# Modulation rows of a two-layer diffusion step: column chunks one by one, or four at a time

## The chip, the cores and the metric

The kernel runs on one core of one Trainium2 chip. The time is the device time of one execution in microseconds (us); the median of several executions counts, and lower is better.

## The reference

One denoising step runs two trunks (128 context tokens and 128 latent tokens of 1024 features) through two layers. Each layer scales and shifts its rows by modulation vectors that come from a conditioning row, mixes the tokens with two recurrences (HGRN2 and mLSTM), adds the result through a gate, normalises, and runs a feed-forward product: a dense SwiGLU in layer 0, a top-2-of-8 mixture of experts in layer 1. Everything is float32. What the change touches is the modulation:

```python
act = jax.nn.silu(cond)
for l in range(DEPTH):
    mod = jnp.einsum('bd,dn->bn', act, w_ada[l]) + b_ada[l]     # w_ada[l]: 1024 x 6144
    sh1, sc1, g1, sh2, sc2, g2 = jnp.split(mod[:, None, :], 6, axis=-1)
    y, states = mixer(x * (1 + sc1) + sh1, ...)
    x = layer_norm(ALPHA * x + g1 * y, ln1_g[l], ln1_b[l])
    hh = x * (1 + sc2) + sh2
    f = swiglu(hh, ...) if l % 2 == 0 else moe_swiglu(hh, ...)
    x = layer_norm(ALPHA * x + g2 * f, ln2_g[l], ln2_b[l])
```

There are two conditioning rows, one for each trunk, so `mod` is a product of 2 rows with a matrix of 24 MB per layer.

## The kernel before, in words

**The large products.** A weight matrix comes from HBM in pieces of 256 rows x 512 columns (tile `ws`, 512 KB, a ring of three buffers). ScalarE (ACT) copies a piece to a rounded part `wh`, VectorE (DVE) subtracts it to get the rest `wl`, and TensorE (PE) takes three products of the two parts with the two parts of the rows (`hTh`, `hTl`) into a bank of PSUM. `gemm_fm` makes 512 output features of both trunks that way with 96 matmuls, `gemm_tm` does it with tokens on the partitions. Every DMA is issued by one queue, SyncE's (SP), in one order: a DMA that waits for its buffer holds back all that stand behind it.

**The modulation rows.** The 6144 columns of `w_ada[l]` are cut into 12 chunks of 512 (`cc` 0 to 11). `ada(l, cc)` makes one chunk. It loads the 1024 rows in four DMAs of 256 rows x 512 columns (tile `wa`, 512 KB; two buffers in pool `wp`, and every third load goes to one more buffer in the pool of the moment, by the list `extra`), and does eight matmuls, one for each tile `kt` of 128 rows. The stationary operand is `actT[:, kt]`, the silu of the conditioning, 32 columns wide of which 2 are used; the moving operand is the 128 x 512 piece of weights. Row tile `kt` goes to column group `kt % 4` of the array, so that each of the four groups (32 columns each, and 32 partitions of the PSUM bank each) holds the sum of two row tiles. `ps` is copied to `part` in SBUF, and four small matmuls (`adT`) with the selector `selc` add the four groups up and turn the chunk to feature-major; VectorE adds the bias and writes `mod`. Of the chunks that are gates (4, 5, 10, 11) the rows stay as rows: one matmul (`adR`) with the selector `selg` adds the groups and the bias row, which a DMA puts into partition 2 of `part`, and two rows of 512 go to HBM.

**When.** The first four chunks of layer 0 are made at the start, from weights loaded whole (`front`). The other 20 stand in the list `todo`; `chunk_done`, called at the end of every `gemm_fm` and `gemm_tm`, takes one entry. In layer 0's mixer there are 17 entries for 24 products, in the dense feed-forward four (chunks 0 to 3 of layer 1), in layer 1's mixer 16. PSUM bank `ad` of pool `adp` is one buffer: `ad`, `adT`, `adR`, the vectors' transposes `rT` and the products `warm` share it in turn. The framework's scheduler then sets the order of the instructions on every engine.

Names in the views: `ad` are the eight matmuls of a chunk, `mm` and `fp` the large products, `pl`, `po` those of the HGRN2 recurrence, `pn`, `pS`, `pqk`, `pC` those of the mLSTM. A float32 matmul stands in the trace as two records.

Of the kernel before, what the change touches and what calls it, by code (L numbers as in the profile page):

```python
# [17 lines left out]
T = 128  # L18
# [23 lines left out]
def backbone(ctx, tc, x_prompt, x_sample, c, state_hgrn, state_mlstm_C, state_mlstm_n, state_mlstm_m,  # L42
# [34 lines left out]
    tt(selg, selc[:, 0:2], ident[:, 2:3].to_broadcast([128, 2]), ALU.add)  # L77

# [66 lines left out]
    # conditioning: silu of both rows, as the stationary operand of the modulation product  # L145
# [7 lines left out]
    # lower bounds of the second layer's forget gates  # L153
# [34 lines left out]
    def sub(out, a, b):  # L188
        """a - b; GpSimd takes the first few after a norm, where the vector engine is what is waited for"""
        if aside[0]:  # L190
            aside[0] -= 1
            G.tensor_tensor(out, a, b, op=ALU.subtract)
        else:
            tt(out, a, b, ALU.subtract)
# [54 lines left out]
    def keep_warm(n, after=None):  # L249
        """Products that nothing reads, so that the array's clock stays up while a norm is waited for"""  # L250
        if not n:
            return
        with tc.issue_after(after or last_mm[0]):
            ps = adp.tile([128, 128], F32, tag="ad", name="warm")
            for _ in range(n):
                mm(ps, ident, ident)
# [3 lines left out]
    def chunk_done():  # L260
        """After a chunk of a product, a chunk of the modulation rows that are due later."""
        if todo:
            nxt = todo.pop(0)
            if callable(nxt):
                nxt()
            elif nxt:
                ada(*nxt)

# [5 lines left out]
    extra = []  # a pool with room for one more chunk  # L274
    chunks = [0]

    def ada_load(l, cc, k, pool=None, bufs=2):
        if extra and not pool:
            chunks[0] += 1
            if chunks[0] % 3 == 0:  # L280
                pool, bufs = extra[0], 1
        st = (pool or wp).tile([128, 2, 512], F32, tag="wa", name="wa", bufs=bufs)
        nc.sync.dma_start(out=st, in_=w_ada[l][k * 128:k * 128 + 256, cc * 512:cc * 512 + 512]
                          .rearrange("(k p) n -> p k n", p=128))
        return st

    def ada(l, cc, whole=None):
        """One chunk of 512 modulation values; the rows' tiles go to the four column groups in turn."""
        ps = whole[1].tile([128, 512], F32, tag="ad", name="ad") if whole else adp.tile([128, 512], F32, tag="ad", name="ad")
        for kt in range(KT):  # L290
            if kt % 2 == 0:
                st = whole[0][kt // 2] if whole else ada_load(l, cc, kt)
            g = kt % 4
            mm(ps[32 * g:32 * g + 32], actT[:, kt, :], st[:, kt % 2], kt < 4, kt >= 4, (0, 32 * g))
        part = wp.tile([128, 512], F32, tag="part", name="part", bufs=1)
        S.copy(part, ps)
        if cc in (4, 5, 10, 11):
            nc.sync.dma_start(out=part[2:3], in_=b_ada[l:l + 1, cc * 512:cc * 512 + 512])
            pf = adp.tile([2, 512], F32, tag="ad", name="adR")
            mm(pf, selg, part)  # L300
            S.copy(part[0:2], pf)
            nc.sync.dma_start(out=gates_d[l][cc // 6][:, (cc % 2) * 512:(cc % 2) * 512 + 512], in_=part[0:2])
            return
        end = None
        pf = (whole[1] if whole else adp).tile([128, 4, 2], F32, tag="xc" if whole else "ad", name="adT")
        for j in range(4):
            end = mm(pf[:, j], part[:, j * 128:j * 128 + 128], selc[:, 0:2])
        if whole and cc == 0:
            vectors(0, v1_first)
        tt(mod[l][:, 4 * cc:4 * cc + 4], pf,  # L310
           v1[l][:, 80 + 4 * cc:84 + 4 * cc, None].to_broadcast([128, 4, 2]), ALU.add)
        return end

    def mod_gb(l, which, g, b, ks=slice(0, 8)):
        """Scale and shift that take the normalised rows to the modulated ones."""
        n = ks.stop - ks.start
        sh = mod[l][:, 24 * which + ks.start:24 * which + ks.stop]
        sc = mod[l][:, 24 * which + 8 + ks.start:24 * which + 8 + ks.stop]
        gs = const.tile([128, n, 2], F32, name=f"gs{l}{which}{ks.start}")
        bs = const.tile([128, n, 2], F32, name=f"bs{l}{which}{ks.start}")  # L320
        V.tensor_scalar(gs, sc, 1.0, None, op0=ALU.add)
        if g is None:
            V.tensor_copy(bs, sh)
        else:
            tt(bs, gs, b[:, :, None].to_broadcast([128, 8, 2]), ALU.mult)
            tt(bs, bs, sh, ALU.add)
            tt(gs, gs, g[:, :, None].to_broadcast([128, 8, 2]), ALU.mult)
        return gs, bs
# [19 lines left out]
    def modulate(src, gs, bs, hm):  # L348
        """hm[feature, tile, trunk, token] = src^T * gs + bs"""
# [35 lines left out]
    def gate_rows(pool, tag, l, which, bufs=1):  # L385
        """A gate of each trunk over all partitions: [token, trunk, feature]"""
        gb = pool.tile([128, 2, D], F32, tag=tag, name="gb", bufs=bufs)
        for tr in range(2):
            nc.sync.dma_start(out=gb[:, tr], in_=bcast_row(gates_d[l][which][tr], D))
        return gb  # L390

    def norm_stats(small, row):
        """Mean and inverse deviation of a row [token, feature]"""
# [7 lines left out]
    def layer_norm(small, pre, trs=(0, 1)):  # L401
        """pre [token, trunk, feature] -> normalised, in place"""
# [6 lines left out]
    def norm_row(pool, tag, ap, bufs=1):  # L409
        """A norm's gain or bias over all partitions"""  # L410
# [15 lines left out]
    # ------------------------------------------------------------------ mixer  # L426
    def mixer(l, rhs, mx, sm, hp, mp, quads):
# [10 lines left out]
        # gates of the memory, rows [head, ...]  # L438
# [94 lines left out]
        def hgrn(g):  # L533
# [44 lines left out]
            def update(l2, ca=0, ck=0, step=1):  # L578
                """Blocks of 2**l2 become blocks of twice the size; of every step-th sequence, from ca and ck."""
# [38 lines left out]
            # outputs, normalised over each head  # L618
# [20 lines left out]
            def states():  # L639
                """Final states of the first trunk"""  # L640
# [25 lines left out]
        def gate_out(pp, y, norm, gate):  # L666
            """y [token, c, v] -> (y^T * norm gain * gate), feature-major, in gate's place"""
# [44 lines left out]
        def mlstm(g, raw, V1):  # L712
# [9 lines left out]
            for j in range(4):  # L722
# [35 lines left out]
                # sums of the gates over all partitions  # L758
# [35 lines left out]
                # final states of the first trunk  # L794
# [12 lines left out]
            # normalise over each head  # L807
# [58 lines left out]
    def residual(z, gb, q4, tr, ps):  # L866
        """z <- ALPHA * x + gate * ps for one half row of a trunk"""
# [4 lines left out]
    def quad(pool):  # L872
        """Two tensors of eight tiles"""
        t_ = pool.tile([128, 2, HC, T], F32, tag="mws", name="quad", bufs=4)
        return t_[:, 0], t_[:, 1]
# [35 lines left out]
    # ------------------------------------------------------------------ layer 0  # L911
    with tc.tile_pool(name="first", bufs=1) as first, tc.tile_pool(name="firstp", bufs=2, space=PSUM) as firstp:
        w_first = {}

        def front(cc):
            w_first[cc] = [ada_load(0, cc, k, first, 16) for k in range(0, KT, 2)]
# [36 lines left out]
        for q4 in range(2):  # L953
            ada(0, q4, (w_first[q4], firstp))
            x_cols(q4)
            end = ada(0, 2 + q4, (w_first[2 + q4], firstp))
# [14 lines left out]
    todo += [lambda: vectors2(0), (0, 4), lower]  # L971
    for cc in range(5, 12):
        todo += [(0, cc), vectors_rest if cc == 5 else None]
    mrhs = mixer_half(0, rhs0)
    assert not todo
    with ExitStack() as es:
# [9 lines left out]
        todo += [(1, cc) for cc in range(4)]  # L986
# [36 lines left out]
    # ------------------------------------------------------------------ layer 1  # L1023
    for cc in range(4, 12):
        todo += [None, (1, cc)]
# [24 lines left out]
    # router  # L1050
# [25 lines left out]
    with tc.high_priority():  # L1076
# [30 lines left out]
        # each token's place in its experts' lists  # L1107
# [5 lines left out]
    # modulated rows, token-major, in two parts  # L1113
# [27 lines left out]
    def park(src, kts, c0, tags=("gh", "gl"), bufs=6):  # L1141
        """Loads into the places of the gated rows that come after them"""
# [11 lines left out]
    def blocks(srcs, nk, c0, n, kinds=()):  # L1154
        """128 rows of n columns of every source at a time, side by side, in two parts"""
# [52 lines left out]
    def before_norm(tr, gate, out, q4):  # L1208
        """ALPHA * x + gate * the experts' sum, for half of a trunk's rows"""
# [5 lines left out]
    def finish(tr, mv, rstd, ng, out):  # L1215
        """The last norm of a trunk's rows"""
# [8 lines left out]
    def expert_weights():  # L1225
        """The chosen experts' weights"""
# [11 lines left out]
    def experts(first_slot):  # L1238
        """The tokens in slots first_slot..first_slot+127 of every expert's list."""
# [4 lines left out]
        def gather(p2):  # L1244
            """The rows of two experts' tokens, feature-major, and the places to put theirs back"""
# [149 lines left out]
```

## Time and profile before

| | |
|---|---|
| times of three executions | 1945.79, 1949.02, 1949.86 us; median 1949.02 |
| span of the profiled execution | 1946.4 us (of its time, the views give the span alone) |
| PE busy | 1882.5 us, 97% of the span |
| DVE busy, ACT busy | 1485.5 us (76%), 1186.7 us (61%) |
| chain that ended last, by engine | PE 91%, DVE 4%, DMA 3%, ACT 1%, issue 1% |
| mean DMA rate | 257 GB/s |

A matmul's end in the trace is modelled, and matmuls overlap; so what a matmul costs is read here from the start of one to the start of the next. A row of the timeline merges equal instructions that follow each other, gives the first one's start, and the time to the last one's end.

In time, the span falls into the start (0 to about 40 us), layer 0's mixer (to about 437), its output product and norm, the dense feed-forward (475 to 615 at its densest, to 693 with the norm), layer 1's mixer (to about 1090), router, and the experts (to the end).

### The profile page before, as it was taken

What the parts mean: (1) busy time and instruction counts of PE and PEld (TensorE: products, weight loads), DVE (VectorE), ACT (ScalarE), POOL (GpSimd) and SP (SyncE); (2) the same over time, 40 slices, a digit from 0 to 9 for tenths busy, and PEclk for the clock granted to TensorE, in tenths of its full rate; (3) what the DMA queues carried; (4) which work ended last, traced back from release to release, by engine and by line L of the source; (5) the groups of instructions that cost most, each with busy time, mean ns of one, the idle gap of its engine ahead of it and who ended that gap; (6) DMA issues with size and microseconds to landing.
All of it is one profiled execution on the core that took longest, in us unless ns stands there. A gap on an engine that the chain in (4) does not pass through costs nothing.

```text
span 1946.4 us, 31146 instructions
## 1 busy us (share of the span) xinstructions
PE 1882.5 (97%) x11942; PEld 1589.7 (82%) x11942; DVE 1485.5 (76%) x2195; ACT 1186.7 (61%) x1527; POOL 79.5 (4%) x77
## 2 busy tenths in 40 slices
PE   8999999997999989999999899999999999999996
PEld 4879788996899877898899778888887888788884
DVE  3488687577445577968967789988988898889887
ACT  3567555643344344775574378777777777678773
POOL 2000000003000020000000300000000000000000
PEclk9999999998999989999999899999999999999998
DMA  9656765555865566677555879999999999999993
GB/s 313 219 192 203 238 193 163 155 179 182 270 196 175 192 200 204 180 227 232 159 153 177 312 263 359 359 325 354 355 339 329 356 361 344 324 331 356 355 341 129
DMA packets 283534, 500.91 MB, mean 257 GB/s; under 512 B 17012, under 2 KB 56520, under 8 KB 283376
## 3 DMA queue, kind: packets, MB, share of 16 engines
q1 hardware_dynamic: 283376, 498.83, 76.2%
q8 instruction: 96, 1.57, 0.3%
q14 instruction: 62, 0.51, 0.1%
HBM read 493.45 MB, written 5.32 MB: 256 GB/s over the span
## 4 chain that ended last, share of the span: by engine, by line
PE 91%; DVE 4%; DMA 3%; ACT 1%; issue 1%; SPq 0%; DVEq 0%; ACTq 0%
PE mm L56 66%; PE fp L56 10%; PE ad L56 4%; PE pl L56 2%; DMA wa<-in_w_ada_dram 2%; PE acc L56 2%; PE pn L56 1%; PE g L1313 1%; PE po L56 1%; PE pqk L56 1%; DVE rs_y L345 1%; PE adT L56 1%; PE g L56 1%; DVE mwl L52 1%; DMA ws<-in_w_out_dram 1%
## 5 line engine op out<-in xcount | busy, mean ns | idle before, releaser
L52 DVE TENSOR_TENSOR mwl<-mws,mwh 128x1024 fp32r<-128x1024 f32 x429 | 513.2, 1222 | 50.0 <-ACT mwh L1202 36.9
L1202 ACT CAST mwh<-mws 128x1024 fp32r<-128x1024 f32 x432 | 445.7, 1051 | 118.5 <-PE mm L56 110.0
L52 DVE TENSOR_TENSOR wl<-ws,wh 128x1024 fp32r<-128x1024 f32 (+1 forms) x268 | 324.4, 1211 | 215.7 <-ACT wh L198 207.0
L198 ACT CAST wh<-ws 128x1024 fp32r<-128x1024 f32 (+1 forms) x278 | 287.4, 1036 | 316.9 <-PE mm L56 173.2
L56 PE MATMUL mm<-hTh,wh 128*128 128x256 f32 x1024 | 294.9, 290 | 3.5 <-ACT hTh L370 1.8
L56 PE MATMUL mm<-hTl,wh 128*128 128x256 f32 x1024 | 293.5, 288 | 2.3 <-DVE hTl L52 2.3
L56 PE MATMUL mm<-hTh,wl 128*128 128x256 f32 x1024 | 291.1, 288 | 0.0
L56 PE MATMUL mm<-mwl,xh 128*128 128x512 f32 x704 | 279.0, 400 | 0.4 <-DVE mwl L52 0.3
L56 PE MATMUL mm<-mwh,xh 128*128 128x512 f32 x704 | 279.0, 396 | 0.0
L56 PE MATMUL mm<-mwh,xl 128*128 128x512 f32 x704 | 278.8, 396 | 0.0
L56 PEld LDWEIGHTS mm<-hTh,wh 128*128 128x128 f32 x1024 | 196.4, 192 | 15.6 <-issue 7.4
L56 PEld LDWEIGHTS mm<-hTh,wl 128*128 128x128 f32 x1024 | 195.9, 193 | 10.4 <-issue 5.9
L56 PEld LDWEIGHTS mm<-hTl,wh 128*128 128x128 f32 x1024 | 197.1, 193 | 7.1 <-issue 3.4
L56 PEld LDWEIGHTS mm<-mwh,xl 128*128 128x128 f32 x704 | 132.5, 188 | 31.6
L56 PEld LDWEIGHTS mm<-mwl,xh 128*128 128x128 f32 x704 | 132.4, 188 | 31.4 <-DVE mwl L52 1.3
L56 PEld LDWEIGHTS mm<-mwh,xh 128*128 128x128 f32 x704 | 132.5, 188 | 30.2
L56 PE MATMUL mm<-mwh,gh 128*128 128x512 f32 x352 | 138.9, 396 | 0.0
L56 PE MATMUL mm<-mwl,gh 128*128 128x512 f32 x352 | 137.9, 394 | 0.6 <-DVE mwl L52 0.6
L56 PE MATMUL mm<-mwh,gl 128*128 128x512 f32 x352 | 137.6, 392 | 0.0
L56 PE MATMUL fp<-hTl,wh 128*128 128x256 f32 x352 | 101.1, 287 | 2.0 <-DVE hTl L52 2.0
L56 PE MATMUL fp<-hTh,wh 128*128 128x256 f32 x352 | 101.0, 287 | 1.1 <-DVE hTh L370 1.1
L52 DVE TENSOR_TENSOR mwl<-ws,mwh 128x1024 fp32r<-128x1024 f32 x74 | 90.1, 1223 | 15.6 <-ACT mwh L1202 13.5
(560 smaller groups left out, 3271.7 us busy)
## 6 DMA issues: line engine op xcount, KB each, us to landing
mws<-in_moe_w_dram SPq DMA_DIRECT2D x202, 1024.0 KB
ws<-in_w_in_dram SPq DMA_DIRECT2D x160, 512.0 KB
wa<-in_w_ada_dram SPq DMA_DIRECT2D x96, 512.0 KB
ws<-in_moe_w_dram SPq DMA_DIRECT2D x70, 512.0 KB
ws<-in_ffn_w_dram SPq DMA_DIRECT2D x62, 512.0 KB
mws<-in_moe_w_dram SPq DMA_DIRECT2D x28, 512.0 KB
ws<-in_w_branch_a_dram SPq DMA_DIRECT2D x16, 512.0 KB
ws<-in_w_branch_b_dram SPq DMA_DIRECT2D x16, 512.0 KB
```

The source lines that it names most:

```text
L52: V.tensor_tensor(out, a, b, op=op)
L56: return PE.matmul(out, lhsT, rhs, start=start, stop=stop, skip_group_check=True, **kw).ins
L198: S.copy(hi, st)
L345: V.scalar_tensor_tensor(y, t, 1.5, y, op0=ALU.add, op1=ALU.mult)
L1202: S.copy(h, t_)
L1313: PE.transpose(ps[:, j], t_[:, j * 128:j * 128 + 128], ident)
```

## The change

The 20 chunks that are made from `todo` are now made four at a time: `ada_quad(l, c4, kt)` works on the 2048 columns of chunks 4*c4 to 4*c4+3 and on one row tile `kt`. It loads two pieces of 128 rows x 1024 columns (512 KB each) and does four matmuls with the same stationary operand `actT[:, kt]`, one per column group, each group being a chunk of its own. Eight calls, one for each row tile, add up in the same PSUM bank (`adq`). The last call copies the bank, and does for all four chunks together what `ada` did for each: four matmuls `adT` with a selector of 8 columns (`sel8`), one addition into `mod` for the chunks that are not gates, and one matmul `adR` with a selector of 4 columns (`sel8b`) for the two chunks that are. The entries of `todo` are 19 in layer 0's mixer (three for vectors first, then 16 calls), 8 in the feed-forward and 18 in layer 1's mixer. The first four chunks of layer 0 stay as they were.

```diff
+    sel8 = const.tile([128, 4, 2], F32, name="sel8")
+    V.tensor_copy(sel8, cap(ident, 0, [[32, 4], [1, 2]]))
+    sel8b = const.tile([128, 4, 2], F32, name="sel8b")
+    tt(sel8b, sel8, cap(ident, 2, [[32, 4], [0, 2]]), ALU.add)
...
             elif nxt:
-                ada(*nxt)
+                ada_quad(*nxt)
...
+    def ada_quad(l, c4, kt):
+        if kt == 0:
+            quad_ps[l, c4] = adp.tile([128, 512], F32, tag="ad", name="adq")
+        ps = quad_ps[l, c4]
+        halves = []
+        for h in range(2):
+            pool, bufs = wp, 2
+            if extra:
+                chunks[0] += 1
+                if chunks[0] % 3 == 0:
+                    pool, bufs = extra[0], 1
+            st = pool.tile([128, 2, 512], F32, tag="wa", name="wa", bufs=bufs)
+            c0 = c4 * 2048 + h * 1024
+            nc.sync.dma_start(out=st, in_=w_ada[l][kt * 128:kt * 128 + 128, c0:c0 + 1024]
+                              .rearrange("p (c n) -> p c n", n=512))
+            halves.append(st)
+        for g in range(4):
+            mm(ps[32 * g:32 * g + 32], actT[:, kt, :], halves[g // 2][:, g % 2], kt == 0, kt == KT - 1, (0, 32 * g))
+        if kt < KT - 1:
+            return
+        part = wp.tile([128, 512], F32, tag="part", name="part", bufs=1)
+        S.copy(part, ps)
+        gs = [(4 * c4 + g) for g in range(4)]
+        gates = [g for g in range(4) if gs[g] in (4, 5, 10, 11)]
+        if len(gates) < 4:
+            pf = adp.tile([128, 4, 4, 2], F32, tag="ad", name="adT")
+            for j in range(4):
+                mm(pf[:, j].rearrange("p g c -> p (g c)"), part[:, j * 128:j * 128 + 128],
+                   sel8.rearrange("p g c -> p (g c)"))
...
+        if gates:
+            for g in gates:
+                cc = gs[g]
+                nc.sync.dma_start(out=part[32 * g + 2:32 * g + 3], in_=b_ada[l:l + 1, cc * 512:cc * 512 + 512])
+            pr_ = adp.tile([4, 512], F32, tag="ad", name="adR")
+            g0 = gates[0]
+            mm(pr_, sel8b[:, g0:g0 + 2].rearrange("p g c -> p (g c)"), part)
+            row = wp.tile([4, 512], F32, tag="part", name="grow", bufs=1)
+            S.copy(row, pr_)
+            for i in range(2):
+                nc.sync.dma_start(out=gates_d[l][c4 - 1][:, i * 512:i * 512 + 512], in_=row[2 * i:2 * i + 2])
...
-    todo += [lambda: vectors2(0), (0, 4), lower]
-    for cc in range(5, 12):
-        todo += [(0, cc), vectors_rest if cc == 5 else None]
+    todo += [lambda: vectors2(0), lower, vectors_rest]
+    todo += [(0, 1 + i // 8, i % 8) for i in range(16)]
...
-        todo += [(1, cc) for cc in range(4)]
+        todo += [(1, 0, kt) for kt in range(KT)]
...
-    for cc in range(4, 12):
-        todo += [None, (1, cc)]
+    todo += [None, None] + [(1, 1 + i // 8, i % 8) for i in range(16)]
```

TensorE's order in the dense feed-forward, before: one chunk (`ad_5240`) is done by a run of six matmuls (row tiles 0 to 5, so groups 0, 1, 2, 3, 0, 1) and, one more piece of `fp` later, a run of two.

```order
L56 MATMUL fp_5119<-hTh_5102,wl_5214 128x256
L56 MATMUL ad_5240<-wa_5241,actT_106 32x512 x2
L56 MATMUL ad_5240<-wa_5245,actT_106 32x512 x2
L56 MATMUL ad_5240<-wa_5249,actT_106 32x512 x2
L56 MATMUL fp_5269<-hTh_5102,wh_5273 128x256
...
L56 MATMUL ad_5240<-wa_5253,actT_106 32x512 x2
L56 MATMUL fp_5270<-hTl_5103,wh_5303 128x256
```

The same engine and stage with the change: one row tile of four chunks (`adq_5210`) at the end of each of eight products, four matmuls in groups 0, 1, 2, 3.

```order
L56 MATMUL fp_5224<-hTh_5072,wl_5319 128x256
L56 MATMUL adq_5210<-wa_5345,actT_110 32x512 x2
L56 MATMUL adq_5210<-wa_5347,actT_110 32x512 x2
L56 MATMUL fp_5359<-hTh_5072,wh_5363 128x256
L56 MATMUL fp_5359<-hTl_5073,wh_5363 128x256
```

The runs of six, in which groups 0 and 1 come twice, are gone there; every run holds each group once.

SyncE's queue in the same stage, before (`wa` are the modulation's loads, `ws` the feed-forward's weights): four loads of a chunk stand around every second product's loads.

```order
L283 DMA wa_5253<-in_w_ada_dram 128x2x512
L283 DMA wa_5392<-in_w_ada_dram 128x2x512
L283 DMA wa_5396<-in_w_ada_dram 128x2x512
L181 DMA ws_5454<-in_ffn_w1_dram 128x2x512
L283 DMA wa_5400<-in_w_ada_dram 128x2x512
L181 DMA ws_5484<-in_ffn_w1_dram 128x2x512
```

With the change:

```order
L187 DMA ws_5361<-in_ffn_w1_dram 128x2x512
L323 DMA wa_5347<-in_w_ada_dram 128x1024
L323 DMA wa_5481<-in_w_ada_dram 128x1024
L187 DMA ws_5391<-in_ffn_w1_dram 128x2x512
L187 DMA ws_5421<-in_ffn_w1_dram 128x2x512
L187 DMA ws_5451<-in_ffn_w1_dram 128x2x512
```

Two loads now stand among each product's four, instead of up to three in a row.

## Rows read from the trace of the kernel before

**Rows 1.** Page: busy time of each engine.

```profile
PE 1882.5 (97%) x11942; PEld 1589.7 (82%) x11942; DVE 1485.5 (76%) x2195; ACT 1186.7 (61%) x1527; POOL 79.5 (4%) x77
```

**Rows 2.** Windows: length, busy (records) of PE, PEld, DVE, ACT, POOL; clock, DMA share, GB/s.

```profile
40.00:437.00 397.00, 393.77 (x3202) 345.18 (x3203) 288.23 (x585) 228.30 (x349) 12.21 (x19) 1.00 0.63 196
475.00:615.00 140.00, 140.00 (x1122) 129.78 (x1122) 66.28 (x77) 59.64 (x73) 0.00 (x0) 0.99 0.64 203
693.00:1048.00 355.00, 351.97 (x2930) 308.68 (x2931) 270.60 (x572) 210.01 (x323) 12.92 (x19) 0.99 0.63 194
86.00:165.00 79.00, 78.04 (x692) 61.76 (x691) 67.88 (x121) 46.28 (x62) 0.02 (x1) 1.00 0.64 206
240.00:306.00 66.00, 66.00 (x595) 51.13 (x594) 57.34 (x118) 30.58 (x42) 0.89 (x3) 1.00 0.62 194
740.00:810.00 70.00, 70.00 (x627) 54.28 (x626) 59.45 (x95) 37.23 (x48) 0.00 (x0) 1.00 0.58 179
890.00:952.00 62.00, 62.00 (x606) 49.78 (x605) 55.35 (x115) 32.25 (x47) 2.10 (x3) 1.00 0.60 190
```

**Rows 3.** Timeline of PE, 235 to 247 us: a run of four matmuls; `adT`.

```profile
236.18 1.06 PE L56 MATMUL ad<-wa,actT 128*32 128x512 f32 x8
237.18 0.50 PE L56 MATMUL mm<-wl,hTh 128*128 128x512 f32 x1
...
240.53 1.04 PE L56 MATMUL ad<-wa,actT 128*32 128x512 f32 x2
241.51 0.69 PE L56 MATMUL pl<-quad,Ks 128*64 128x64 f32 x16
...
245.89 0.95 PE L56 MATMUL adT<-selc,part 128*128 128x2 f32 x8
246.71 0.36 PE L56 MATMUL mm<-hTh,wh 128*128 128x256 f32 x1
```

**Rows 4.** Timeline of PE, 266 to 269 us: a run of six matmuls.

```profile
266.45 0.28 PE L56 MATMUL mm<-hTh,wh 128*128 128x256 f32 x1
266.57 0.28 PE L56 MATMUL mm<-hTl,wh 128*128 128x256 f32 x1
266.78 1.91 PE L56 MATMUL ad<-wa,actT 128*32 128x512 f32 x12
268.62 0.39 PE L56 MATMUL mm<-hTh,wl 128*128 128x256 f32 x1
268.84 0.28 PE L56 MATMUL mm<-hTh,wh 128*128 128x256 f32 x1
```

**Rows 5.** Timeline of PE, 111 to 113 us: a gate's `adR`.

```profile
111.33 1.02 PE L56 MATMUL adR<-part,selg 128*2 128x512 f32 x2
112.28 0.38 PE L56 MATMUL mm<-hTh,wh 128*128 128x256 f32 x1
```

**Rows 6.** Tile `g`, PE, 1120 to 1124 us: the router's turn by 8 columns.

```profile
L56 PE MATMUL g<-selc,part x4: 256/256/277, 1122.4 to 1122.7; 128*128 128x8 f32 x4
```

**Rows 7.** Timeline of PE, 136 to 139 us: the longest wait for a `wa` load.

```profile
137.97 1.05 PE L56 MATMUL ad<-wa,actT 128*32 128x512 f32 x4 [0.86 <-DMA wa<-in_w_ada_dram]
```

**Rows 8.** Waits of SyncE's queue (line waited for: us, times, longest): layer 0's mixer, layer 1's mixer.

```profile
SPq L283 <- PE ad L56: 41.0, 22, 4.8
...
SPq L283 <- PE ad L56: 24.1, 16, 4.0
```

**Rows 9.** Timeline of PE's weight loads, 236 to 237 us.

```profile
236.18 0.16 PEld L56 LDWEIGHTS ad<-wa,actT 128*32 128x32 f32 x8 [0.35 <-issue]
```

**Rows 10.** Tile `ad` on PE by window (busy, records): the four HGRN2 stretches.

```profile
86.00:165.00 79.00, 9.08 (x44) 1.00 0.64 206
240.00:306.00 66.00, 9.25 (x34) 1.00 0.62 194
740.00:810.00 70.00, 8.42 (x34) 1.00 0.58 179
890.00:952.00 62.00, 7.83 (x42) 1.00 0.60 190
```

More of the change, by code (lines that the diff above doesn't have):

```diff
@@ L275, in backbone, with ada_load @@
     chunks = [0]
[L277 to L282, printed above, removed]
+    def ada_load(l, cc, k, pool):
+        st = pool.tile([128, 2, 512], F32, tag="wa", name="wa", bufs=16)
         nc.sync.dma_start(out=st, in_=w_ada[l][k * 128:k * 128 + 256, cc * 512:cc * 512 + 512]
@@ L285, in ada_load, with ada @@
         return st
-    def ada(l, cc, whole=None):
-        ps = whole[1].tile([128, 512], F32, tag="ad", name="ad") if whole else adp.tile([128, 512], F32, tag="ad", name="ad")
+    def ada(l, cc, parts, pool):
+        ps = pool.tile([128, 512], F32, tag="ad", name="ad")
         for kt in range(KT):
-            if kt % 2 == 0:
-                st = whole[0][kt // 2] if whole else ada_load(l, cc, kt)
             g = kt % 4
-            mm(ps[32 * g:32 * g + 32], actT[:, kt, :], st[:, kt % 2], kt < 4, kt >= 4, (0, 32 * g))
+            mm(ps[32 * g:32 * g + 32], actT[:, kt, :], parts[kt // 2][:, kt % 2], kt < 4, kt >= 4, (0, 32 * g))
         part = wp.tile([128, 512], F32, tag="part", name="part", bufs=1)
         S.copy(part, ps)
[L297 to L303, printed above, removed]
         end = None
-        pf = (whole[1] if whole else adp).tile([128, 4, 2], F32, tag="xc" if whole else "ad", name="adT")
+        pf = pool.tile([128, 4, 2], F32, tag="xc", name="adT")
         for j in range(4):
             end = mm(pf[:, j], part[:, j * 128:j * 128 + 128], selc[:, 0:2])
-        if whole and cc == 0:
+        if cc == 0:
             vectors(0, v1_first)
@@ L312, in ada @@
         return end
+    quad_ps = {}
+    def ada_quad(l, c4, kt):
[27 more added lines that the diff above has]
+                   sel8.rearrange("p g c -> p (g c)"))
+            at = [g for g in range(4) if g not in gates]
+            g0, n = at[0], len(at)
+            tt(mod[l][:, 4 * (4 * c4 + g0):4 * (4 * c4 + g0 + n)].rearrange("p (g j) c -> p g j c", j=4),
+               pf[:, :, g0:g0 + n].rearrange("p j g c -> p g j c"),
+               v1[l][:, 80 + 4 * (4 * c4 + g0):80 + 4 * (4 * c4 + g0 + n)]
+               .rearrange("p (g j) -> p g j", j=4)[:, :, :, None].to_broadcast([128, n, 4, 2]), ALU.add)
+        if gates:
[9 more added lines that the diff above has]
+                nc.sync.dma_start(out=gates_d[l][c4 - 1][:, i * 512:i * 512 + 512], in_=row[2 * i:2 * i + 2])
@@ L915, in front @@
         def front(cc):
-            w_first[cc] = [ada_load(0, cc, k, first, 16) for k in range(0, KT, 2)]
+            w_first[cc] = [ada_load(0, cc, k, first) for k in range(0, KT, 2)]
         def x_half(q4):
@@ L953, in backbone @@
         for q4 in range(2):
-            ada(0, q4, (w_first[q4], firstp))
+            ada(0, q4, w_first[q4], firstp)
             x_cols(q4)
-            end = ada(0, 2 + q4, (w_first[2 + q4], firstp))
+            end = ada(0, 2 + q4, w_first[2 + q4], firstp)
             keep_warm((12, 12)[q4], end)
```

## The prediction

> **What bounds the kernel now.** The page comes first: PE is busy 97% of the span [rows 1]. As a matmul's end is modelled, that alone proves little, so the windows come next. The change lives in three stretches, the two mixers and the dense feed-forward, and there PE is busy 393.77 of 397 us, 140.00 of 140 and 351.97 of 355, at a granted clock of 0.99 to 1.00 (the full level, 2.4 GHz), while VectorE has 71 to 76% in the mixers and the DMA engines 0.63 [rows 2]. Then the timeline shows that the starts follow each other without holes: ordinary products of 256 columns start 0.12 us apart [rows 4], and the longest wait for one of the modulation's loads is 0.86 us [rows 7]. So in these stretches PE's own work sets the end, and a microsecond of PE work that is taken out is a microsecond less, as long as nothing else comes late.
>
> **What a modulation matmul costs.** It is a price by run, not by matmul. A lone `ad` matmul (two records) holds PE from 240.53 to 241.51, 0.98 us; four matmuls in the four column groups (eight records) hold it from 236.18 to 237.18, 1.00 us [rows 3]. Different groups overlap nearly whole; a second turn of the same groups does not: six matmuls (twelve records) hold it from 266.78 to 268.62, 1.84 us [rows 4]. So a run costs 0.98 us for its first turn of groups and 0.86 for a second.
>
> **The products.** In the order before, the 160 matmuls of the 20 chunks stand in 53 runs; 14 of them (five or six matmuls) need a second turn. That is 39 x 0.98 + 14 x 1.84 = 64.0 us. With the change the 160 matmuls stand in 54 runs, of which two need a second turn, because most calls of four keep together and hold each group once: 52 x 0.98 + 2 x 1.84 = 54.6 us. Gain 9.4 us. In the feed-forward alone a chunk was a run of six and one of two, 2.82 us, times four; now it is eight runs of four, 7.9 us against 11.3.
>
> On that price the Trainium skill, page "TensorE: Matmul & The Clock Gate", Part 3, says the opposite: weight loads overlap matmuls in flight only when the row group differs, and here all rows are used by every matmul. By that rule four column groups would go one after the other before and after, and this term would be nothing instead of 9.4. Here eight weight loads go by within 0.16 us, beside the matmuls of the other groups [rows 9], so the row decides.
>
> **The turns.** Each of the 12 chunks that are not gates has four `adT` matmuls, 245.89 to 246.71, 0.82 us [rows 3]. Now five groups of four do it. They are 8 columns wide instead of 2; the router's same turn with 8 columns takes 256 ns a record [rows 6], where the 2-column ones last 0.95 us for eight overlapping records [rows 3], and its starts stand as close, so I price them alike; were each to take its 256 ns alone, a group would cost 2.05 us and the term would be 9.8 - 10.2, nothing. I take 7 x 0.82 = 5.7 us, since in both cases it is the load of 128 x 128 of `part` that paces.
>
> **The gates.** Eight `adR` at 0.95 us (111.33 to 112.28 [rows 5]) become four of twice the rows and the same 512 columns: 3.8 us. From below, twice the rows could cost twice, and the term were zero; `ad` matmuls of 32 rows cost the same 0.98 as this one of 2, so I keep 3.8.
>
> **Going in and out.** The matmul ahead of a run starts 0.21 us before it and the one behind takes 0.22 to the next, against 0.12 [rows 4]; 0.19 us for each run of `ad` or `adR`, of which there are 61 before and 58 after: 0.6 us.
>
> **What costs nothing.** The loads: 80 of 512 KB before and after, from rows of 4 KB instead of 2, same issues on SP. The bias rows and gate rows: eight and eight DMAs, as before. ScalarE has 15 copies of `part` and four of the rows fewer, VectorE seven additions; both are off the path, covered by PE's products, and only get shorter. The two new constants are small VectorE instructions ahead of the first `ad`, which waits for its loads.
>
> **The sum.** 9.4 + 5.7 + 3.8 + 0.6 = 19.5 us. Against it I set 2 us of new waits: a new order always has a few; the one before has some too [rows 7]. That leaves 17.5: the span goes from 1946.4 to 1928.9. The median of the runs shown lies 2.6 above that span, so the time goes from 1949.0 to **1931.5**.
>
> **What is late next.** A chunk's bank `ad` was passed on every two products or so; now it is held for eight calls, and then copied, turned, added and read again before the next four chunks may begin. Nothing else asks for it meanwhile: the vectors' transposes now come first, and the warming products and the norm's transposes stand where no call is open. The modulation is also finished later, at the 19th and 18th of 24 products in the mixers instead of the 16th, still ahead of the output product that needs the gates.
>
> **Rivals.**
> *The recurrences keep their time.* In the four HGRN2 stretches VectorE is busy 57 to 68 us of 62 to 79, 85 to 89% [rows 2]: if its chain sets their length, the PE work taken out there only leaves holes. Of the 64.0 us of `ad` some 34.6 lie there (9.08 + 9.25 + 8.42 + 7.83 [rows 10]), so about half of the 17.5 would be lost: 1949.0 - 8.7 = 1940. For it: that load. Against it: PE is busy for 100% in three of the four, and the large products that stand beside the chain need VectorE themselves and can go elsewhere.
>
> *The queue stands (slower).* SP's loads of `wa` wait for `ad` to free their buffer, already 41.0 + 24.1 us in the mixers [rows 8], and the weights of the large products stand behind them. A call now needs two loads at once where three buffers exist. If each of the 32 calls in the mixers ran into a wait as long as the one of 0.86 us [rows 7] plus a going in and out, about 1.05, they would cost 33 us and outweigh 19.5: 1962. It decides from 0.6 us a call on. Against it: in the order with the change the loads stand well ahead of their use, and before, where up to three stood in a row, waits of that size were single ones.
>
> *The groups don't overlap, or the change does not do what it says.* If the column groups did not work side by side when they share the same stationary rows (before, each had its own), a run of four would cost 0.98 + 3 x 0.86 = 3.56 us and the products 142 us instead of 64.0: 1949 + 78 - 10 = 2017. And if column groups never overlapped, as the products stood before too, the first term falls away: 1949 - 10 + 2 = 1941. By the rule of the Trainium skill quoted above, the second of these is what would come; the trace bears it out nowhere. What speaks against both is the run of four [rows 3, 9].
>
> **How the numbers follow.** Likeliest is the sum, 1931.5, with 0.76; what a run varies by, new waits between nothing and 6 us, and the `adT` price spread it from 1926 to 1938. The recurrences keeping their time, 1940, has 0.15; the queue, 1962, 0.05; column groups that share or never overlap 0.02 together; 0.02 is left for a gain of less than 4 us in other ways. Eight in ten lie from **1926 to 1942**. A measurement of this kernel tells about 0.2%, 4 us, from no change: faster by more 0.92, within it 0.03, slower 0.05.
>
> **What would show it.** Right: on PE some 54 runs of `adq`, nearly all with a start-to-next-start of 1.0 us, and five groups of `adT` at 0.8; the feed-forward shorter by about 5.9 us (3.4 of products, 2.4 of turns, 0.1 else), as it is the cleanest of the three; the experts' part as long as before; waits of PE in the mixers still a few us. Wrong: runs of four that last 2 us or more, PE idle for several us at a time in 86 to 306 or 740 to 952 with VectorE as releaser (the first rival), or with a DMA of `ws` or `wa` as releaser and SP held at L323 for more than 65 us (the second).

## The result, and the profile after

The changed kernel takes 1930.79 us (median of four executions, 1929.09 to 1931.87) against 1949.44 in the same comparison: a ratio of 0.9903 [0.9889, 0.9917]. The prediction was 1931.5, faster. Measured a second time, beside the experiments c2 to c4, it took 1931.43, ratio 0.9912 [0.9897, 0.9927]. The two profiled executions span 1930.1 and 1927.4 us, and a single stage differs by up to 1.5 us between them (layer 0's mixer, in the table of stages below).

The page of the kernel after, span and busy times [rows 1]:

```profile
span 1930.1 us, 30972 instructions
PE 1865.4 (97%) x11878; PEld 1581.8 (82%) x11878; DVE 1484.0 (77%) x2190; ACT 1177.6 (61%) x1508; POOL 81.9 (4%) x77
```

PE has 64 records fewer (28 fewer of `adT` matmuls and four fewer of `adR`, two records each) and is busy 17.1 us less; the span is 16.3 shorter. The windows of the same three stretches, after [rows 2]:

```profile
40.00:426.00 386.00, 383.62 (x3181) 340.14 (x3182) 285.88 (x583) 227.16 (x343) 15.15 (x19) 1.00 0.65 200
465.00:605.00 140.00, 139.17 (x1124) 130.39 (x1124) 67.36 (x75) 60.68 (x73) 0.00 (x0) 0.99 0.68 211
678.00:1033.00 355.00, 352.89 (x2938) 310.85 (x2939) 273.20 (x572) 205.59 (x315) 12.22 (x19) 0.99 0.63 196
```

PE is idle for 2.4, 0.8 and 2.1 us there; before it was 3.2, 0 and 3.0. It is still PE's own work that sets the end, and apart from one wait of 0.8 us in the feed-forward (below) no new wait took the place of the work removed.

The timeline of PE after: one `adR` of four rows, and in the feed-forward a run of four column groups, the `adT` matmuls of four chunks, and the weight loads of the run [rows 3, 5, 9]:

```profile
366.89 1.02 PE L56 MATMUL adR<-part,sel8b 128*4 128x512 f32 x2
367.85 0.39 PE L56 MATMUL mm<-hTl,wh 128*128 128x256 f32 x1
...
488.29 0.28 PE L56 MATMUL fp<-hTh,wl 128*128 128x256 f32 x1
488.50 1.06 PE L56 MATMUL adq<-wa,actT 128*32 128x512 f32 x8
489.50 0.38 PE L56 MATMUL fp<-hTh,wh 128*128 128x256 f32 x1
...
569.87 0.96 PE L56 MATMUL adT<-sel,part 128*128 128x8 f32 x8
570.68 0.36 PE L56 MATMUL fp<-hTl,wh 128*128 128x256 f32 x1
```

```profile
488.50 0.16 PEld L56 LDWEIGHTS adq<-wa,actT 128*32 128x32 f32 x8
```

The run of four holds PE for 1.00 us, the turn of all four chunks for 0.81, the two gates together for 0.96. Each is as long as the same run was for one chunk. Summed over all runs from their starts in the two traces (us; runs in brackets):

| | before | after | predicted |
|---|---|---|---|
| products `ad`, `adq` | 64.1 (53) | 55.1 (54) | 64.0 to 54.6 |
| turns `adT` | 9.9 | 4.0 | -5.7 |
| gates `adR` | 7.6 (8) | 3.8 (4) | -3.8 |

And by stage, each from the start of its first large product to that of the next stage, in the profiled executions (c1 is the kernel with the change again; c4, d2, d3 and d4 are other experiments, below):

| us | before | after | c1 | c4 | d2 | d3 | d4 |
|---|---|---|---|---|---|---|---|
| layer 0's mixer | 407.4 | 396.8 | 395.3 | 391.2 | 386.7 | 382.0 | 420.8 |
| its output and norm | 38.6 | 38.5 | 39.2 | 37.3 | 37.0 | 38.3 | 39.6 |
| feed-forward, first part | 147.6 | 143.2 | 142.6 | 142.9 | 135.7 | 135.6 | 159.4 |
| feed-forward, rest and norm | 75.8 | 75.7 | 75.7 | 75.7 | 75.8 | 75.3 | 75.7 |
| layer 1's mixer | 385.9 | 382.7 | 382.2 | 375.7 | 378.8 | 368.8 | 406.6 |
| its output and the router | 52.5 | 52.1 | 51.6 | 51.6 | 53.0 | 53.2 | 52.3 |
| experts | 814.8 | 817.3 | 817.3 | 817.5 | 816.0 | 815.2 | 815.7 |

The gain comes from the three stages that hold the modulation, as forecast: 10.6 + 4.4 + 3.2 = 18.2 in the first profile, and 12.1 + 5.0 + 3.7 = 20.8 in the second. The experts, which the change doesn't touch, give 2.5 back.

**The feed-forward** was to show 5.9. Its products went from 11.3 to 8.0 and its turns from 3.2 to 0.8, which is 5.7; one new wait at the end of the stage takes part of it back. Waits of PE after, 459 to 605 us:

```profile
PE fp L56 <- ACT wh L204: 0.8, 1, 0.8
```

Why that one piece of weights is rounded late was not followed further. In the second profile of the same kernel the stage is 142.6, so 5.0 us are gained there, though the wait is there too (0.7 us).

**The experts.** Their work is the same to the instruction (3548 matmul records from the first to the last). What differs is the granted clock behind two waits of PE, both while the experts' rows are gathered and until VectorE's `xl` is done. Windows after, and before, at the same two places (us from the start, then the columns of [rows 2]); the first row of each holds the first wait:

```profile
1473.00:1478.00 5.00, 2.14 (x15) 1.66 (x14) 5.00 (x7) 3.74 (x7) 0.00 (x0) 1.00 1.05 388
1478.00:1481.00 3.00, 3.00 (x13) 2.71 (x13) 2.28 (x5) 1.34 (x3) 0.00 (x0) 0.51 1.05 385
...
1682.00:1686.00 4.00, 4.00 (x17) 3.61 (x16) 2.96 (x5) 1.45 (x3) 0.00 (x0) 0.50 1.01 331
```

```profile
1492.00:1497.00 5.00, 2.14 (x16) 1.66 (x15) 5.00 (x7) 3.74 (x7) 0.00 (x0) 1.00 1.05 376
1497.00:1500.00 3.00, 3.00 (x18) 2.49 (x17) 2.21 (x5) 2.00 (x4) 0.00 (x0) 1.00 1.04 388
...
1699.50:1703.50 4.00, 4.00 (x17) 3.49 (x16) 2.92 (x5) 1.57 (x4) 0.00 (x0) 0.65 0.92 320
```

The waits themselves are alike. After, and before, at the first place:

```profile
1476.65 0.39 PE L56 MATMUL mm<-sel,hhh 128*128 128x256 f32 x1 [2.86 <-DVE xl L1305]
...
1495.58 0.39 PE L56 MATMUL mm<-sel,hhh 128*128 128x256 f32 x1 [2.86 <-DVE xl L1264]
```

At the second place PE is idle for 3.60 us in both kernels. At the first it is busy from the wait on; before, the clock stays at its full level, 2.4 GHz, and after, it is at the half one, 1.2 GHz, for about 3 us. At the second place it is low for longer than before. Counted from the experts' first product, PE is 1.3 us later than before when the second wait ends, and 2.5 at the end of the span.

### The profile page after: what moved, and what is told of

Its sections match the earlier page's. It is cut to its first block, busy times and chain, and to the rows that moved or that the text cites. A ratio compares the mean times of both kernels' runs of the same rounds, so it can differ in the third digit from the quotient of the medians.

```text
span 1930.1 us, 30972 instructions
## 1 busy us (share of the span) xinstructions
PE 1865.4 (97%) x11878; PEld 1581.8 (82%) x11878; DVE 1484.0 (77%) x2190; ACT 1177.6 (61%) x1508; POOL 81.9 (4%) x77
## 4 chain that ended last, share of the span: by engine, by line
PE 91%; DVE 5%; DMA 2%; ACT 1%; issue 1%; SPq 0%; DVEq 0%; ACTq 0%
PE mm L56 67%; PE fp L56 10%; PE adq L56 3%; PE pl L56 2%; PE acc L56 2%; PE pn L56 1%; PE g L1354 1%; PE po L56 1%; PE pqk L56 1%; DVE rs_y L388 1%; DMA wa<-in_w_ada_dram 1%; PE g L56 1%; DVE mwl L52 1%; DMA ws<-in_w_out_dram 1%; PE ad L56 0%
## 5 line engine op out<-in xcount | busy, mean ns | idle before, releaser
L52 DVE TENSOR_TENSOR mwl<-mws,mwh 128x1024 fp32r<-128x1024 f32 x429 | 513.7, 1222 | 51.9 <-ACT mwh L1243 39.2
```

The lines of the kernel that those rows point to most:

```text
L52: V.tensor_tensor(out, a, b, op=op)
```

## The experiments

All are variants of the kernel after, except c2, which is the kernel before with its modulation in other pieces. Those with c ran with one set of runs of the kernel before (1949.27), those with d with another (1948.35).

**c1: the kernel with the change again.**

> The changed kernel as it is, beside the others. Measured 1930.8 us against 1949.4 before. If the experts' part, 2.5 us longer in its trace than before (817.3 against 814.8 us from the first expert product to the end), is a spread between executions, it will differ here by about as much; if the change moved something there, it will be 817 again.

Measured: 1931.43 us, and the experts 817.3 us long as in the first profile. By what was expected, the 2.5 us are then not a mere spread between executions (of the kernel before there is one profile, with 814.8); what in the change moved them stays open, as the edit doesn't touch that stage. c1 is what c3 and c4 are held against.

**c2: short runs alone.** Chunks one by one as before, but each in two calls of four matmuls, one per column group, at the end of two products. The entries for the vectors come first, as in the change. Turns and gates stay as they were before.

```diff
-                ada(*nxt)
+                ada_half(*nxt)
...
+        for kt in range(4 * h, 4 * h + 4):
             if kt % 2 == 0:
+                st = ada_load(l, cc, kt)
             g = kt % 4
             mm(ps[32 * g:32 * g + 32], actT[:, kt, :], st[:, kt % 2], kt < 4, kt >= 4, (0, 32 * g))
```

> Only the run part of the change: a chunk stays alone, but is made in two calls of four matmuls (row tiles 0 to 3, then 4 to 7), one call per product, with two loads each; turns and gates stay 20 times as before. In the order the 160 matmuls stand in 51 runs of four or fewer. Theory (PE time, priced by run): products 51 x 0.985 = 50.2 us against 64.0, in and out two runs fewer, so 1949.4 - 14 = 1935. Rival (the gain comes from ScalarE's and VectorE's copies and additions that fall away, and from PE's queue waiting for them): nothing is gained, 1949.

Measured: 1935.78 us, ratio 0.9928 [0.9914, 0.9942]. Its products stand in 51 runs, none of more than four matmuls, and hold PE for 50.5 us by the trace, 13.6 less than before; the time is 13.5 less. So short runs without a second turn are worth 13.5 us by themselves, and need no accumulation of four chunks in one bank. That is more than the 9.0 us that the products gave in the change: there the two second turns and three more runs cost 4.6 us of it, and about half of the change's gain comes from turns and gates. The sum holds for the kernel and not for each stage: in c2's profile layer 0's mixer is 10.6 us shorter for 7.1 us of products less, and layer 1's is 1.3 longer for 3.1 less.

**c3: turns and gates chunk by chunk again.** Products as in the change; after the copy, four `adT` or one `adR` for each chunk.

```diff
-        if len(gates) < 4:
-            pf = adp.tile([128, 4, 4, 2], F32, tag="ad", name="adT")
+        for g in range(4):
+            cc = gs[g]
...
+            pf = adp.tile([128, 4, 2], F32, tag="ad", name="adT")
+            for j in range(4):
+                mm(pf[:, j], part[:, j * 128:j * 128 + 128], sel8[:, g])
```

> The changed kernel with the turns and gates made chunk by chunk again (12 groups of adT with 2 columns, 8 adR with 2 rows), from the one bank of four chunks. The runs of products stay (54). Theory: 5.9 us of adT and 3.8 of adR come back, 1930.8 + 10 = 1941. Rival (turns and gates hide, the products made the whole gain): 1931. Second rival (their copies and additions on ScalarE and VectorE cost too): above 1944.

Measured: 1939.71 us, ratio 0.9958 [0.9945, 0.9972], 8.3 more than c1. In its trace `adT` takes 9.9 us again instead of 4.0 and `adR` 7.6 instead of 3.8, together 9.7 more. In its profile the experts take 816.1 us, 1.2 less than in c1, which is most of what lies between 8.3 and 9.7. The terms for turns and gates hold. A wider selector and more rows of the result cost nothing.

**c4: the four matmuls of a call kept together.** A call's matmuls need two loads, and in the change the 40 calls stand in 54 runs, many of them split. Here the two matmuls of the second load come first and the others follow at once.

```diff
-        for g in range(4):
-            mm(ps[32 * g:32 * g + 32], actT[:, kt, :], halves[g // 2][:, g % 2], kt == 0, kt == KT - 1, (0, 32 * g))
+        end = None
+        for g in (2, 3, 0, 1):
+            with ExitStack() as es:
+                if end:
+                    es.enter_context(tc.issue_after(end))
+                    es.enter_context(tc.high_priority())
+                end = mm(ps[32 * g:32 * g + 32], actT[:, kt, :], halves[g // 2][:, g % 2], kt == 0, kt == KT - 1, (0, 32 * g))
```

> The changed kernel with the four matmuls of a call kept together on PE: they start with the second load's, and the other three follow at once. 40 runs of four instead of 54 runs. Theory: products 40 x 1.0 = 40 us instead of 55.1, 14 fewer times in and out at 0.19, so 1930.8 - 18 = 1913. Rival (what the scheduler broke up it broke up because the second load is late, and PE now waits for it; or the recurrences keep their time): 1925 to 1931, with waits of PE for wa in the trace.

Measured: 1917.11 us, ratio 0.9838 [0.9824, 0.9851], the fastest complete version here: 14.3 less than c1. There are 40 runs, each of four groups, and they hold PE for 39.8 us instead of 55.1; with 14 runs fewer at 0.19 us of going in and out that would be 18.0. Windows of its two mixers:

```profile
40.00:415.00 375.00, 370.00 (x3158) 335.49 (x3159) 279.51 (x577) 224.00 (x338) 12.48 (x19) 1.00 0.65 205
671.00:1026.00 355.00, 351.61 (x2999) 316.91 (x2999) 277.77 (x579) 211.57 (x320) 14.68 (x19) 0.99 0.63 200
```

PE is idle for 5.0 and 3.4 us instead of 2.4 and 2.1. These 3.9 us account for the 3.7 between 18.0 and what came: the first sign that the chains of other engines are no longer far behind.

**d1: rows of 2 KB.** The change also made the rows of a load 4 KB long. Here a load takes chunks `g` and `g + 2`, so its rows are 2 KB again.

```diff
-            c0 = c4 * 2048 + h * 1024
-            nc.sync.dma_start(out=st, in_=w_ada[l][kt * 128:kt * 128 + 128, c0:c0 + 1024]
-                              .rearrange("p (c n) -> p c n", n=512))
+            c0 = c4 * 2048
+            nc.sync.dma_start(out=st, in_=w_ada[l][kt * 128:kt * 128 + 128, c0:c0 + 2048]
+                              .rearrange("p (c h n) -> p h c n", h=2, n=512)[:, h])
...
-            mm(ps[32 * g:32 * g + 32], actT[:, kt, :], halves[g // 2][:, g % 2], kt == 0, kt == KT - 1, (0, 32 * g))
+            mm(ps[32 * g:32 * g + 32], actT[:, kt, :], halves[g % 2][:, g // 2], kt == 0, kt == KT - 1, (0, 32 * g))
```

> The changed kernel with the loads' rows in HBM of 2 KB as before: a load takes chunks 0 and 2, or 1 and 3, of the four, so that two rows of 512 columns lie 1024 apart. Same bytes, same number of loads, 53 runs of products. Theory (PE's work alone): 1930 to 1932. Rival (the longer rows brought part of it): 1935 or more.

Measured: 1931.32 us, ratio 0.9909 [0.9893, 0.9926]; c1 was 1931.43. The longer rows did not bring the 4 us or more of the rival. That they brought nothing is not shown: d1's experts take 814.6 us, 2.7 less than in c1, which can hide as much elsewhere. The three stages with the modulation add up to 923.6 us in its profile, against 922.7 and 920.1 in the two of the change, so that longer rows are worth up to some 3 us is not excluded. Why the experts are shorter, the windows at the same two places say:

```profile
1480.00:1483.00 3.00, 3.00 (x19) 2.53 (x19) 2.39 (x5) 1.99 (x4) 0.00 (x0) 1.00 1.05 387
...
1682.00:1686.00 4.00, 4.00 (x21) 3.39 (x20) 2.68 (x5) 2.60 (x4) 0.00 (x0) 0.98 1.02 357
```

The clock does not fall at the first and is back sooner at the second, where the wait is shorter as well, after the change (first row) 3.60 us and in d1 2.21:

```profile
1680.19 0.58 PE L56 MATMUL mm<-sel,hhh 128*128 128x256 f32 x1 [3.60 <-DVE xl L1305]
...
1678.92 0.58 PE L56 MATMUL mm<-sel,hhh 128*128 128x256 f32 x1 [2.21 <-DVE xl L1305]
```

Over all ten profiles it goes together: where the clock stayed at full level at the first place the experts took 814.6 to 815.2 us (before, d1, d3), where it fell, 815.7 to 817.5 (the other seven). At the first place the wait is 2.86 us in all ten; at the second it is 2.21 in d1 and d4, and 3.6 in the others.

**d4: one column group.** The matmuls of row tiles 1 to 6 all go to column group 0, so that in six of every eight calls no two matmuls have different groups. The number of matmuls and the loads are the same; the modulation values are other ones.

```diff
         for g in range(4):
-            mm(ps[32 * g:32 * g + 32], actT[:, kt, :], halves[g // 2][:, g % 2], kt == 0, kt == KT - 1, (0, 32 * g))
+            o = g if kt in (0, KT - 1) else 0
+            mm(ps[32 * o:32 * o + 32], actT[:, kt, :], halves[g // 2][:, g % 2], kt == 0, kt == KT - 1, (0, 32 * o))
```

> The changed kernel with the four matmuls of row tiles 1 to 6 all in column group 0 instead of the four groups (the modulation is not that of the reference): the same matmuls, loads and number of runs. Theory (groups overlap, turns of the same group don't): 120 matmuls at 0.86 us and 0.12 for each run, about 108 us instead of 39, so 1930.8 + 69 = 2000. Rival (column groups do not overlap anyhow): 1931.

Measured: 1993.59 us, ratio 1.0227 [1.021, 1.0244]. The timeline of PE shows a run of four in one group:

```profile
263.92 3.62 PE L56 MATMUL adq<-wa,actT 128*32 128x512 f32 x8
267.48 0.39 PE L56 MATMUL mm<-hTh,wh 128*128 128x256 f32 x1
```

It holds PE for 3.56 us, where four groups take 1.00: 0.98 + 3 x 0.86, the price that the prediction gave to groups that do not overlap. Over all runs the products take 65.5 us more than after the change, and the span is 63.5 longer. So the overlap of column groups is what is paid for. (A group is 32 columns of the array and 32 partitions of the bank; d4 moves both, so which of the two paces is not shown.) The rule of the Trainium skill, page "TensorE: Matmul & The Clock Gate", Part 3, that weight loads overlap only when the row group differs, taken alone as the prediction took it, would have made this kernel and c1 equal; the measurement decides against it for column groups. But that the skill says the opposite of the price, as the prediction has it, was too narrow a reading: the same Part of that page lists three matmuls in three column groups as 2.38 times faster, and here four groups take 1.00 us against 3.56.

**d2: products of row tiles 1 to 6 left out, loads kept.** 30 of 40 calls have no matmuls; their weights are still loaded. The question is how much further down the PE work can go.

```diff
-        for g in range(4):
+        for g in range(4) if kt in (0, KT - 1) else ():
```

> The changed kernel without the matmuls of row tiles 1 to 6 (30 of 40 calls); their loads stay, so the modulation is not that of the reference. 40 matmuls remain in 16 runs. Theory (a microsecond of PE work taken out is a microsecond less): 55.1 - 16.5 = 38.6 us of products and 38 times in and out at 0.19, 1930.8 - 46 = 1885. Rival (the recurrences keep their time): half of the mixers' share stays, 1904 or so.

Measured: 1908.35 us, ratio 0.9796 [0.9778, 0.9815]. The straight sum misses by 23 us, and the rival is nearer. In the trace the products hold PE for 16.6 us instead of 55.1 and there are 38 runs fewer, so PE's own work is some 45.7 less; the span is only 23.6 shorter than after the change. Windows of the two mixers of d2:

```profile
40.00:410.00 370.00, 360.68 (x3059) 332.85 (x3060) 279.79 (x576) 219.41 (x335) 13.76 (x19) 1.00 0.68 218
659.00:1014.00 355.00, 341.77 (x2877) 314.84 (x2877) 273.49 (x576) 216.63 (x324) 12.49 (x19) 0.98 0.62 198
```

PE is idle for 9.3 and 13.2 us, against 2.4 and 2.1 after the change: 18.0 us of the 22.1 that are missing; the other 4.1 were not traced. The waits of PE there, layer 0's mixer and then layer 1's:

```profile
PE pC L56 <- DVE kts L842: 2.1, 2, 1.4
PE mm L56 <- ACT so L751: 2.0, 1, 2.0
...
PE mm L56 <- ACT wh L204: 1.6, 1, 1.6
PE mm L56 <- ACT KK L589: 1.2, 1, 1.2
...
PE pk L56 <- DVE quad L835: 3.6, 2, 3.2
PE mm L56 <- ACT so L751: 3.2, 1, 3.2
```

None of the mixers' waits of PE after the change is one of these. The timeline of ACT in d2 ahead of the wait of 3.2 us (PE stood until `so` was there, at 787.5):

```profile
780.54 1.28 ACT L812 ACT_TABLE_LOAD   x1
781.84 1.15 ACT L812 ACTIVATE w<-w 128x512 f32<-128x512 f32 x2
782.89 0.59 ACT L775 ACTIVATE acc<-quad,v 128x256 f32<-128x256 f32 x1
783.39 1.06 ACT L673 ACTIVATE sq<-po 128x512 f32<-128x512 f32 x2
784.34 1.04 ACT L204 CAST wh<-ws 128x1024 fp32r<-128x1024 f32 x1
785.40 1.28 ACT L751 ACT_TABLE_LOAD   x1
786.70 0.84 ACT L751 ACTIVATE so<-mm,v 128x256 f32<-128x256 f32 x2
```

ScalarE works through these seven microseconds without a hole, for three different parts (the mLSTM's `w` and `acc`, the recurrence's `sq`, a weight piece's `wh`), with two table loads of 1.28 us among them, and PE stands for the last of it. In the feed-forward, which has no recurrence, the same edit gave 7.5 us: eight runs became three, which is 5 x (1.00 + 0.19) = 6.0 by the straight sum, and 0.8 is the wait after the change, which d2 does not have: 6.8 together.

**d3: the loads of those row tiles left out too.**

```diff
         ps = quad_ps[l, c4]
+        if kt not in (0, KT - 1):
+            return
         halves = []
```

> As the run without the matmuls of row tiles 1 to 6, and their 60 loads (30 MB) left out too; the modulation is not that of the reference. Theory (the loads are hidden): as that run within 3 us, 1885. Rival (the loads hold the queue, and with it the weights of the large products): lower by 6 us or more.

Measured: 1893.49 us, ratio 0.9714 [0.9698, 0.973], 14.9 less than d2: the rival's outcome. The mixers are 4.7 and 10.0 us shorter than in d2, the feed-forward the same. In d2 SP's queue waits for the former load of the same buffer; its row for layer 0's mixer:

```profile
SPq L323 <- DMA wa<-in_w_ada_dram: 60.6, 27, 6.8
```

For layer 1's mixer it is 37.1. After the change these waits were 5.7 and 2.2. In d3 it is 1.1 us in layer 0's mixer and nothing in the other, and none of the waits of PE shown above is left. Which of two costs of the loads decides, SP's standing or the bandwidth they take from the weights of the large products, d2 and d3 do not separate.

## Why the prediction was right

**The run as the price.** Right: a run of four groups takes 1.00 us, a second turn of a group 0.84 to 0.86 more, and the loss of the overlap costs what was computed (d4). The products fell by 9.0 us; 9.4 was said, and c2 shows the term alone. The change doesn't have fewer runs, 54 against 53; it has shorter ones.

**Turns and gates.** 5.9 and 3.8, against 5.7 and 3.8, and c3 gives 8.3 of these 9.7 back in the time of the whole kernel. The 8-column turn was bounded between 0.82 and 2.05 us and lies at the lower end, 0.81.

**In and out.** The 0.6 us can't be seen alone. In layer 0's mixer the other three terms make 8.1 us and the stage lost 10.6; by the sums from the starts the recurrences' `pl` and `yT` and the large products `mm` take 1.2, 0.9 and 0.6 less, and they are broken up less often (`pl` in 22 runs instead of 27, `yT` in 14 instead of 20). In layer 1's mixer the terms make 4.9 and the stage lost 3.2. What evened out between the two was not predicted.

**The 2 us of new waits.** As a total they came out right, and that is luck: the 2 was set by judgement, no row gave its size, and what took the time was for the most part not a new wait. The three stages with the modulation gained 18.2 and 20.8 us in the two profiles, about the whole 19.5 of the sum. The mixers have less idle PE time than before, the feed-forward got one wait of 0.8, and the larger loss is in the experts, 2.5 us through the granted clock. The prediction said that their part would be as long as before: that sentence was wrong, and what took the 2.5 was not a wait but the granted clock after waits that were there already.

**The rivals.** The recurrences did not keep their time: PE is idle less than before. (VectorE's least busy of the four stretches has 55.35 us [rows 2], not the 57 that the prediction reads; the shares are right.) But the mechanism is real and lies close: c4 loses 3.9 of its 18.0 us to idle PE time, and d2 18.0 of 45.7. It begins just below the time that the change reached. SP's queue stood for `adq` longer in sum than before, 34.0 and 44.4 us in the two mixers against 41.0 and 24.1 [rows 8], and PE did not wait for a load of `wa` once; with the products gone (d2), the loads do cost time. The queue's rows after the change, layer 0's mixer and layer 1's:

```profile
SPq L323 <- PE adq L56: 34.0, 16, 6.0
...
SPq L323 <- PE adq L56: 44.4, 16, 6.0
```

Of the sign that the prediction named for the second rival one half came, SP held for more than 65 us; the other, PE idle behind a DMA, did not. That groups sharing their rows do not overlap is excluded by the run of four.

## What to carry to other kernels

In this kernel small stationary operands are priced by the turn, not by the matmul: put matmuls into different column groups, issue each group once, and keep such a run together, since every split adds a whole turn and a going in and out. If several results lie in the groups of one bank, turn them all with one wider selector, as the passes over the 128 x 128 parts are then shared. And when a stretch is bound by PE for 99%, the straight sum held here for what was taken out first (19.3 us of work; the time fell by 18.7 and 17.8 in two comparisons), less so for the next (14.3 of 18.0 in c4), and by about half in d2 (23.6 of 45.7): look at which engine's chain ends next before promising more.

## What the runs showed that was not expected

- The same wait of PE (2.86 us) was followed by about 3 us at the half clock in seven profiles and by the full clock in three, where PE's instructions are the same; both traces of the kernel with the change show the half clock. A stage that no edit touched differs by up to 2.9 us with it (814.6 to 817.5).
- A float32 matmul of 512 columns and 32 rows of result holds its own column group for about 0.86 us, as (3.56 - 0.98) / 3 in d4 says, and leaves the other three free nearly whole.
- Loads that no matmul reads still cost 14.9 us (d2 against d3), although the DMA share in d2's mixers is 0.62 to 0.68.
